# Binding the single-block split of a seven-product pair behind the split of the tile before it

## The chip, the cores and the metric

The kernel runs on one core of one Trainium2 chip. The metric is device time in microseconds (us) of one execution, given as the median of several executions. Of one execution there is also a profile, taken by the hardware profiler, from which all durations below come.

## The reference

One decoder layer in float32, on 272 tokens (16 meta tokens and 256 of the sequence) of width 2048. Two SwiGLU feed-forward blocks stand around a merge of a differential-attention mixer and a short convolution:

```
s = s + 0.5 * swiglu(rms_norm(s), ffn1)            # 2048 -> 2 x 5632 -> 2048
h = rms_norm(s);  q, k, v, b, c, u = split(h @ w_in)
gates = sigmoid(h @ w_gate)                        # 2048 -> 2 x 2048
merged = gates[0] * (y_att @ w_branch[0]) + gates[1] * (y_conv @ w_branch[1])
s = s + merged @ w_out
s = s + 0.5 * swiglu(rms_norm(s), ffn2)            # gate, up = split(h @ w_gu); (silu(gate) * up) @ w_down
return rms_norm(s)[16:]
```

The change touches how weights are prepared for `w_gate` and for ten of the eleven column groups of the second feed-forward's `w_gu`.

## The kernel before

**Precision by splitting.** TensorE multiplies in a reduced format (float32r). To keep float32 accuracy every operand is split into a high and a low part, and each product is made of three matmuls: high times high, low times high, high times low. For weights the split is done by `parts` (L384): ScalarE (ACT) casts the loaded weights to the high part `wh` (L392), and VectorE (DVE) subtracts to get the low part `wl` (L393). A "tile" below is one such split: 128 partitions by two blocks of 512 columns (a wide tile), or by one block of 512 (the single block).

**Direct and seven-product pairs.** `linear_mix` (L483) multiplies the activations, 256 tokens, by two column groups of 512. It goes through the 2048 rows of the weight in eight pairs of 128-row chunks. A direct pair (kind D) is eight products in two wide tiles, each with four products, so 12 matmuls for each tile. A seven-product pair (kind S) uses the Winograd form of Strassen's scheme: seven products on sums of blocks, in four tiles, in this order (L567 to L572):

- the single block, one product (3 matmuls),
- a wide tile of two loaded blocks, two products (6 matmuls),
- `t24`, two sums made on DVE by `sum24` (L538, L539), two products,
- `t13`, two sums, two products; in the second feed-forward they are made by an accumulating DMA on the GpSimd queue (`prefetch`, L543), in the gates by DVE (L531).

The kinds are `DDDSDSDS` for the gates (four passes of `linear_mix`) and `DDSDSSDS` for the second feed-forward (ten passes, column groups 1 to 10, taken in three groups of 3, 4 and 3 with the down projection behind each). That makes 12 and 40 single blocks, 52 in all.

**Buffers.** Loaded weights of a pair go into `st`, four buffers, by two DMAs on the SyncE (SP) queue (L526). The wide tiles' `wh` and `wl` rotate through three buffers each, so a wide cast can only start when TensorE has finished with the tile three places before. The single block has buffers of its own (tag `sc`, two buffers, one for `wh` and one for `wl`), so it doesn't wait for that rotation.

**What sets the order.** The program's text is not the order in which the engines run. A planner lays out each engine's queue from costs of its own: an instruction whose operands and buffers it takes to be ready goes ahead of earlier ones that still wait. On the chip each engine then runs its queue in that order. `tc.issue_after(ins)` binds: every instruction traced inside the block is put behind `ins` in the queue of `ins`'s engine. It was used here for `sum24` (L579), bound behind a given tile's subtraction. Matmuls are traced two wide tiles behind the splits (`step`, L246, AHEAD = 2).

At the end of a pass the eight PSUM results are combined on ACT and DVE (`done`, L588: L591 and L596 copy on ACT, L601 to L612 on DVE), and then SiLU and product (L622, L623). At the start of the next pass this work shares the two queues with the next pass's splits.

Of the kernel before, what the change touches and what calls it, by code (L numbers as in the profile page):

```python
# [9 lines left out]
F32 = mybir.dt.float32  # L10
# [41 lines left out]
def decoder_layer(ctx: ExitStack, tc: tile.TileContext, t, out):  # L52
    nc = tc.nc
# [46 lines left out]
    def load_gain(g0, src):  # L100
# [5 lines left out]
        out=vrows[G_CONV:G_SUB, :], in_=t["conv_w"][0].rearrange("k (c p) -> (k c) p", p=P)  # L106
# [3 lines left out]
    for i, n in enumerate(("lambda_q1", "lambda_k1", "lambda_q2", "lambda_k2")):  # L110
# [7 lines left out]
        out=mask[:, T - P :],  # L118
        in_=mask[:, T - P :],
# [126 lines left out]
    def step(use, ring=True):  # L246

        ahead.append((use, ring))
        while sum(r for _, r in ahead) > AHEAD:
            ahead.pop(0)[0]()  # L250
# [71 lines left out]
    def linear_tok(ops, chunks, k0, name, evict, side_at=(5, 9, 13), hold=0, after=None):  # L322
# [46 lines left out]
        for b, c in enumerate(chunks):  # L369
            if b % 2 == 0:  # L370
                st = wpool.tile([P, 2, 2, GW], F32, tag="st", bufs=ST_BUFS, name="st")
                r0 = (k0 + c) * P
                rows = [w[r0 : r0 + 2 * P, :].rearrange("(c p) f -> p c f", p=P) for w in (w0, w1)]
                if w1 is w0 and c1 == c0 + GW:
                    nc.sync.dma_start(out=st.rearrange("p c q f -> p c (q f)"), in_=rows[0][:, :, c0 : c0 + 2 * GW])
                else:
                    for q, cq in enumerate((c0, c1)):
                        nc.sync.dma_start(out=st[:, :, q, :], in_=rows[q][:, :, cq : cq + GW])
            wh, wl = parts(st[:, b % 2], held=b >= nk - hold)
            step(lambda b=b, wh=wh, wl=wl: use(b, wh, wl))  # L380

    split_last = [None]

    def parts(src, n=2, held=False):  # L384

        wh, wl = (
            tmp.tile([P, 1, GW], F32R, tag="sc", name=nm) if n == 1
            else (apool.tile([P, 2, GW], F32R, tag="act", name=nm) if held else wpool.tile([P, 2, GW], F32R, tag=nm, name=nm))
            for nm in ("wh", "wl")
        )  # L390
        wh, wl = wh[:, :n, :], wl[:, :n, :]
        nc.scalar.copy(out=wh, in_=src)  # L392
        split_last[0] = nc.vector.tensor_sub(wl, src, wh.bitcast(F32)).ins  # L393
        return wh, wl

    ng = F // GW
# [86 lines left out]
    def linear_mix(a, w, cols, name, done, fetch):  # L483
# [25 lines left out]
        def use(p, n, products):  # L509

            for k, left_op, wh, wl in products:
                product(k, left_op, wh, wl)
            if p == a.turn_at and later:
                later.pop(0)()
            if n == (1 if kinds[p] == "D" else 3):
                if p == 0:
                    flush()
                if side:
                    side.pop(0)()

        def load(p):

            st = wpool.tile([P, 2, 2, GW], F32, tag="st", bufs=ST_BUFS, name="st")
            rows = w[2 * p * P : (2 * p + 2) * P, :].rearrange("(c p) f -> p c f", p=P)
            for q in range(2):
                nc.sync.dma_start(out=st[:, :, q, :], in_=rows[:, :, cols[q] : cols[q] + GW])  # L526
            t13 = t24 = None
            if kinds[p] == "S":
                if not fetch:
                    t13 = wpool.tile([P, 2, GW], F32, tag="tt", bufs=2, name="t13")  # L530
                    nc.vector.tensor_add(t13, st[:, 0, :, :], st.rearrange("p c q f -> p q c f")[:, 1, :, :])  # L531
                t24 = wpool.tile([P, 2, GW], F32, tag="tt", bufs=2, name="t24")
            return st, t13, t24

        def sum24(k):
            st, t13, t24 = loaded[k]
            t13 = fetched.get(k, t13)
            nc.vector.tensor_add(t24[:, 0, :], t13[:, 0, :], st[:, 1, 1, :])  # L538
            nc.vector.tensor_add(t24[:, 1, :], t24[:, 0, :], st[:, 1, 0, :])  # L539
# [3 lines left out]
        def prefetch(p):  # L543
            t13 = fetched[p] = aux.tile([P, 2, GW], F32, tag="act", name="t13")
            rows = w[2 * p * P : (2 * p + 2) * P, :].rearrange("(c p) (q f) -> p c q f", p=P, q=2)
            fs = slice(cols[0], cols[0] + GW)
            nc.gpsimd.dma_start(out=t13, in_=rows[:, 0, :, fs])
            nc.gpsimd.dma_start(out=t13, in_=rows[:, :, 1, fs], accum_op=ALU.add)
# [3 lines left out]
        for p, kind in enumerate(kinds):  # L552
            if fetch:
                for k in range(0 if p == 0 else p + 4, min(p + 5, len(kinds))):
                    if kinds[k] == "S":
                        prefetch(k)
            st, t13, t24 = loaded[p]
            t13 = fetched.get(p, t13)
            (a11, a21), (a12, a22) = ([a.block(2 * p + c, i) for i in range(2)] for c in range(2))
            if kind == "D":  # L560
                tiles = [
                    (st[:, c], (("2", a1, 0), ("3", a1, 1), ("4", a2, 0), ("x", a2, 1)))
                    for c, (a1, a2) in enumerate(((a11, a21), (a12, a22)))
                ]
            else:
                s1, s2, s3, s4 = a.sums[p]
                tiles = [  # L567
                    (st[:, 1, 1:2, :], (("3", s4, 0),)),
                    (st[:, :, 0, :], (("1", a11, 0), ("2", a12, 1))),
                    (t24, (("6", s2, 0), ("4", a22, 1))),  # L570
                    (t13, (("5", s1, 0), ("7", s3, 1))),
                ]  # L572
            for n, (src, products) in enumerate(tiles):
                if n == 1 and p + far < len(kinds):
                    loaded[p + far] = load(p + far)
                wh, wl = parts(src, src.shape[1])
                if (p, n) in a.sums_at:

                    with tc.issue_after(split_last[0]):  # L579
                        sum24(a.sums_at[p, n])  # L580
                products = [(k, left_op, wh[:, j, :], wl[:, j, :]) for k, left_op, j in products]
                step(lambda p=p, n=n, products=products: use(p, n, products), src.shape[1] > 1)

    def mixed(a, w, cols, name, end, fetch=False):
# [3 lines left out]
        def done(k, ps):  # L588
# [21 lines left out]
            elif k == "7":  # L610
# [3 lines left out]
                pending.append(lambda: end(gt, up))  # L614

        linear_mix(a, w, cols, name, done, fetch)

    def gate_up_mix(a, w_gu, g, m, gi):
# [397 lines left out]
    for half in thirds:  # L1016
# [10 lines left out]
        if final:  # L1027
            for q in range(2):
                nc.gpsimd.dma_start(
                    out=gfin[q],  # L1030
                    in_=t["norm_final"][q * W2 : (q + 1) * W2].rearrange("(o d) -> o d", o=1).to_broadcast([P, W2]),
# [53 lines left out]
```

## Time and profile before

| quantity | value |
|---|---|
| time, median of 3 executions (range) | 2219.99 us (2218.17 to 2220.8) |
| time of the profiled execution | 2218.36 us |
| its span, first to last instruction | 2216.6 us (1.76 us lie around it) |
| mean granted TensorE clock | 0.996 |
| busy PE, DVE, ACT, POOL | 2183.6, 1469.3, 1058.2, 81.5 us |
| data moved | 443.91 MB, 200 GB/s on average |
| gates with their branch products | about 1122 to 1350 us of the span |
| ten passes of the second feed-forward, with the down projections | about 1500 to 2216 us |

How to read it: PE is TensorE's matmuls, PEld its weight loads. In a timeline row stand the start, the duration, the engine, the line, the operation, what is written and read, the shape, and in brackets how long the engine had been idle before it and what ended that. In a windows row stand a stretch, its length, the busy time and number of instructions of PE, PEld, DVE, ACT and POOL, then the granted TensorE clock, the mean busy share of the 16 DMA engines, and GB/s. A wait row names who waited for whom, us in total, how often, and the longest.

### The profile page before, as it was taken

The numbers are of one execution on the slowest core, as the hardware profiler recorded it, in microseconds if no ns is written. First come the engines' busy times: TensorE is split into PE (matmuls) and PEld (weight loads), VectorE is DVE, ScalarE is ACT, GpSimd is POOL, SyncE is SP. The second block draws the span as 40 slices with busy tenths as digits, with TensorE's granted clock in tenths as the row PEclk, the third lists the DMA queues.
The fourth block names the chain that finished last, engine by engine and source line by source line (L and its number), as shares of the span: only waits on it lengthen the run. The fifth ranks groups of instructions, "written<-read, shape, count | busy, mean of one in ns | idle before, by whom it ended". The sixth has DMA issues, their size and how long they took to land.

```text
span 2216.6 us, 33340 instructions
## 1 busy us (share of the span) xinstructions
PE 2183.6 (99%) x13504; PEld 1974.0 (89%) x13504; DVE 1469.3 (66%) x1919; ACT 1058.2 (48%) x1322; POOL 81.5 (4%) x97
## 2 busy tenths in 40 slices
PE   9999999999999999999999999999999999999998
PEld 8999999999999999898988888888778877887786
DVE  7555554455555565667897777679795678846885
ACT  6343343333433443444455555556563455534554
POOL 0000000000000000000000001000110011101100
PEclk9999999999999999999999999999999999999999
DMA  7455554555545555444555558556996699967973
GB/s 253 171 173 178 180 174 172 172 176 180 176 171 172 175 176 182 152 134 153 171 203 196 190 198 257 176 185 216 277 280 214 220 279 271 281 200 239 270 248 118
DMA packets 209034, 443.91 MB, mean 200 GB/s; under 512 B 9972, under 2 KB 10160, under 8 KB 208880
## 3 DMA queue, kind: packets, MB, share of 16 engines
q1 hardware_dynamic: 191232, 397.97, 52.4%
q0 software_dynamic: 17184, 43.16, 8.4%
q8 instruction: 105, 1.72, 0.3%
q10 hardware_dynamic: 464, 0.66, 0.1%
q14 instruction: 49, 0.40, 0.1%
HBM read 439.65 MB, written 2.10 MB: 199 GB/s over the span
## 4 chain that ended last, share of the span: by engine, by line
PE 92%; DMA 4%; DVE 2%; ACT 1%; issue 1%; SPq 0%; DVEq 0%; ACTq 0%
PE pg L505 4%; PE pu L297 4%; PE pd L297 4%; PE pd L295 4%; PE pu L295 4%; PE pu L296 4%; PE pd L296 4%; PE pg L504 4%; PE pg L503 4%; PE pg L297 4%; PE pg L295 4%; PE pg L296 4%; PE pd L337 4%; PE pd L335 4%; PE pd L336 4%; DMA st<-in_ffn_w_gu_dram 4%
## 5 line engine op out<-in xcount | busy, mean ns | idle before, releaser
L284 DVE TENSOR_TENSOR wl<-st,wh 128x1024 fp32r<-128x1024 f32 x392 | 478.9, 1224 | 453.3 <-ACT wh L283 452.8
L283 ACT CAST wh<-st 128x1024 fp32r<-128x1024 f32 x392 | 411.3, 1050 | 609.8 <-PE pd L296 146.9
L393 DVE TENSOR_TENSOR wl<-st,wh 128x1024 fp32r<-128x1024 f32 (+1 forms) x360 | 409.6, 1143 | 145.0 <-ACT wh L392 144.1
L392 ACT CAST wh<-st 128x1024 fp32r<-128x1024 f32 (+1 forms) x360 | 354.5, 991 | 300.1 <-PE pd L336 111.1
L295 PE MATMUL pg<-h,wh 128*128 128x272 f32 x704 | 203.0, 289 | 1.1 <-ACT wh L283 1.1
L295 PE MATMUL pu<-h,wh 128*128 128x272 f32 x704 | 203.2, 289 | 0.0
L297 PE MATMUL pu<-h,wl 128*128 128x272 f32 x704 | 203.1, 288 | 0.0
L297 PE MATMUL pd<-m,wl 128*128 128x272 f32 x704 | 203.0, 288 | 0.0
L295 PE MATMUL pd<-m,wh 128*128 128x272 f32 x704 | 203.0, 288 | 0.0
L296 PE MATMUL pd<-m,wh 128*128 128x272 f32 x704 | 202.5, 288 | 0.0
L296 PE MATMUL pu<-h,wh 128*128 128x272 f32 x704 | 202.4, 288 | 0.0
L296 PE MATMUL pg<-h,wh 128*128 128x272 f32 x704 | 201.8, 288 | 0.0
L297 PE MATMUL pg<-h,wl 128*128 128x272 f32 x704 | 200.5, 289 | 0.9 <-DVE wl L284 0.9
L393 DVE TENSOR_TENSOR wl<-t,wh 128x1024 fp32r<-128x1024 f32 x104 | 126.7, 1224 | 62.9 <-ACT wh L392 60.3
L392 ACT CAST wh<-t 128x1024 fp32r<-128x1024 f32 x104 | 108.6, 1051 | 122.9 <-PE pgx L504 76.2
L503 PE MATMUL pg<-wh,hn 128*128 128x512 f32 x360 | 143.3, 398 | 15.3 <-ACT wh L392 15.3
L505 PE MATMUL pg<-wl,hn 128*128 128x512 f32 x360 | 143.5, 399 | 4.4 <-DVE wl L393 4.4
L504 PE MATMUL pg<-wh,hn 128*128 128x512 f32 x360 | 142.3, 395 | 0.0
L335 PE MATMUL pd<-wh,m 128*128 128x512 f32 x352 | 137.6, 391 | 0.0
L337 PE MATMUL pd<-wl,m 128*128 128x512 f32 x352 | 137.1, 389 | 0.0
L336 PE MATMUL pd<-wh,m 128*128 128x512 f32 x352 | 137.0, 389 | 0.0
L295 PEld LDWEIGHTS pg<-h,wh 128*128 128x128 f32 x704 | 132.3, 188 | 1.8 <-ACT wh L283 1.8
(305 smaller groups left out, 4854.7 us busy)
## 6 DMA issues: line engine op xcount, KB each, us to landing
st<-in_ffn_w_gu_dram SPq DMA_DIRECT2D x184, 512.0 KB, 5.0
st<-in_ffn_w_down_dram SPq DMA_DIRECT2D x88, 1024.0 KB, 5.1
st<-in_ffn_w_gu_dram SPq DMA_DIRECT2D x84, 1024.0 KB, 4.9
st<-in_w_in_dram SPq DMA_DIRECT2D x48, 1024.0 KB, 5.1
t<-in_ffn_w_gu_dram POOLq DMA_DIRECT2D x80, 512.0 KB, 6.6
st<-in_w_gate_dram SPq DMA_DIRECT2D x64, 512.0 KB, 4.3
st<-in_w_branch_dram SPq DMA_DIRECT2D x32, 512.0 KB, 5.3
st<-in_w_out_dram SPq DMA_DIRECT2D x16, 1024.0 KB, 5.0
```

The source lines that it names most:

```text
L283: nc.scalar.copy(out=wh[:, :m, :], in_=sw)
L284: nc.vector.tensor_sub(wl[:, :m, :], sw, wh[:, :m, :].bitcast(F32))
L295: nc.tensor.matmul(a, wh[:, i, f], act.part(c, 0, t0, t1), start=first, stop=False)
L296: nc.tensor.matmul(a, wh[:, i, f], act.part(c, 1, t0, t1), start=False, stop=False)
L297: nc.tensor.matmul(a, wl[:, i, f], act.part(c, 0, t0, t1), start=False, stop=last)
L335: nc.tensor.matmul(ps, hi, wh[:, q, :], start=first, stop=False)
L337: nc.tensor.matmul(ps, hi, wl[:, q, :], start=False, stop=last)
L392: nc.scalar.copy(out=wh, in_=src)
L393: split_last[0] = nc.vector.tensor_sub(wl, src, wh.bitcast(F32)).ins
L503: nc.tensor.matmul(ps[k], hi, wh, start=first, stop=False)
L504: nc.tensor.matmul(ps[k], lo, wh, start=False, stop=False)
L505: nc.tensor.matmul(ps[k], hi, wl, start=False, stop=left[k] == 0)
```

## The change

`parts` keeps the last tile's two instructions (the cast on ACT and the subtraction on DVE) in `part_last`. When the tile is a single block (`n == 1`), its cast and its subtraction are traced with `issue_after` on both: the cast goes behind the preceding tile's cast on ACT, and the subtraction behind the preceding tile's subtraction on DVE. Nothing else is bound anew: `sum24` stays bound to the same subtraction under its new name. No instruction, buffer or transfer is added or taken away.

```
-    split_last = [None]
+    part_last = []
 
     def parts(src, n=2, held=False):
...
-        nc.scalar.copy(out=wh, in_=src)
-        split_last[0] = nc.vector.tensor_sub(wl, src, wh.bitcast(F32)).ins
+        with ExitStack() as order:
+            if n == 1 and part_last:
+
+                for ins in part_last:
+                    order.enter_context(tc.issue_after(ins))
+            part_last[:] = [nc.scalar.copy(out=wh, in_=src).ins]
+            part_last.append(nc.vector.tensor_sub(wl, src, wh.bitcast(F32)).ins)
         return wh, wl
...
-                    with tc.issue_after(split_last[0]):
+                    with tc.issue_after(part_last[1]):
                         sum24(a.sums_at[p, n])
```

## The prediction

> **What bounds the kernel now.** I read the page first: the span and the engines.
>
> ```profile
> span 2216.6 us, 33340 instructions
> PE 2183.6 (99%) x13504; PEld 1974.0 (89%) x13504; DVE 1469.3 (66%) x1919; ACT 1058.2 (48%) x1322; POOL 81.5 (4%) x97
> ```
>
> PE is the bound, and no work of PE's is removed. So the change can only be worth what PE loses now: idle time, and time at a lower clock. Next, therefore, the table of waits of PE, and of the stretch 1480 to 2100 for ACT:
>
> ```profile
> PE pg L503 <- ACT wh L392: 15.3, 7, 2.8
> PE pg L505 <- DVE wl L393: 4.4, 7, 0.7
> ...
> ACT wh L392 <- DMA st<-in_ffn_w_gu_dram: 27.7, 10, 4.1
> ```
>
> PE waits for weight splits seven times, 15.3 + 4.4 = 19.7 us. Both lines lie in `linear_mix`, and the splits are of `parts`. In the same stretch ACT waits for loads ten times. Whether the one makes the other is seen in the timelines of ACT and of PE around one such wait:
>
> ```profile
> 1820.33 1.05 ACT L392 CAST wh<-t 128x1024 fp32r<-128x1024 f32 x1 [1.71 <-PE pgx L504]
> 1823.05 1.05 ACT L392 CAST wh<-t 128x1024 fp32r<-128x1024 f32 x1 [1.67 <-PE pgx L504]
> 1824.00 0.58 ACT L591 COPY u2x<-pgx 128x512 f32<-128x512 f32 x1
> 1827.53 0.62 ACT L392 CAST wh<-st 128x512 fp32r<-128x512 f32 x1 [2.95 <-DMA st<-in_ffn_w_gu_dram]
> 1828.06 0.58 ACT L596 COPY cup<-pg 128x512 f32<-128x512 f32 x1
> 1828.53 2.94 ACT L392 CAST wh<-st 128x1024 fp32r<-128x1024 f32 x3
> 1833.40 1.06 ACT L392 CAST wh<-st 128x1024 fp32r<-128x1024 f32 x1 [1.93 <-PE pgx L504]
> ```
>
> ```profile
> 1824.64 0.39 PE L504 MATMUL pg<-wh,hn 128*128 128x512 f32 x1
> ...
> 1825.55 0.39 PE L505 MATMUL pg<-wl,sp 128*128 128x512 f32 x1
> ...
> 1827.36 0.39 PE L504 MATMUL pg<-wh,sp 128*128 128x512 f32 x1
> 1827.59 0.39 PE L505 MATMUL pg<-wl,sp 128*128 128x512 f32 x1
> 1829.63 0.50 PE L503 MATMUL pg<-wh,hn 128*128 128x512 f32 x1 [1.66 <-ACT wh L392]
> 1829.97 0.39 PE L504 MATMUL pg<-wh,hn 128*128 128x512 f32 x1
> 1830.20 0.40 PE L503 MATMUL pg<-wh,hn 128*128 128x512 f32 x1
> 1831.26 0.50 PE L505 MATMUL pg<-wl,hn 128*128 128x512 f32 x1 [0.67 <-DVE wl L393]
> 1831.59 0.40 PE L504 MATMUL pg<-wh,hn 128*128 128x512 f32 x1
> ```
>
> The 128x512 cast is a single block. It belongs to the third pair of the pass that starts here (the first S of `DDSDSSDS`), and it stands ahead of the four wide casts of the two direct pairs before it (the x3 row and the one at 1833.40). Its load landed only at 1827.5, so ACT stood for 2.95 us while the first direct tile, which PE needs first, was queued behind. That the three wide casts then run back to back, with no wait, shows that their data and buffers had been ready. So PE's wait is made by order alone.
>
> **What one such wait costs.** Matmuls follow each other every 0.23 us (1827.36 to 1827.59), though a row shows 0.39. From 1827.59 to 1829.63 are 2.04 us where 0.23 is due: 1.81 lost, against 1.66 shown as idle. The next interval, 0.34, loses 0.11; 1830.20 to 1831.26 loses 0.83, and the one after it (0.33) 0.10. That is 2.85 lost for 2.33 shown, 0.5 more. Over seven: 19.7 + 7 x 0.5 = 23.2 us.
>
> Then the clock. The windows view, asked for the 3.41 us shortly after four of the seven waits (first, last and sum of the four):
>
> ```profile
> 1565.89:1569.30 3.41, 3.41 (x10) 2.65 (x9) 3.41 (x5) 0.92 (x1) 0.43 (x1) 0.50 0.76 242
> ...
> 2098.37:2101.78 3.41, 3.04 (x7) 2.48 (x8) 3.41 (x6) 0.58 (x1) 0.00 (x0) 0.50 0.88 237
> sum 13.64, PE 12.33 PEld 9.28 DVE 13.64 ACT 3.57 POOL 0.43; mean PE 3.08 PEld 2.32 DVE 3.41 ACT 0.89 POOL 0.11
> ```
>
> ```profile
> 1566.44 0.63 PE L504 MATMUL pg<-wh,hn 128*128 128x512 f32 x1
> 1566.87 0.63 PE L505 MATMUL pg<-wl,hn 128*128 128x512 f32 x1
> ```
>
> The granted clock is 0.50 there, and matmuls come every 0.43 us instead of 0.23: 47% of PE's busy time is lost, 12.33 x 0.47 = 5.8 us. So the waits and their aftermath cost 23.2 + 5.8 = 29.0 us.
>
> The Trainium skill ("TensorE: Matmul & The Clock Gate", Why this matters for your kernels) sees a danger to the clock only in idle gaps of over about 3 us. By that rule gaps of 2.8 us and less would leave the clock alone, and the sum would be 23.2. The rows disagree, so the measurement decides; the 3.41 us itself is what the page gives as the length of the gate's window.
>
> **The change part by part.** *The bind on ACT.* At the seven places the single goes behind the fourth wide cast. The wide casts then start when their buffers come free. The rotation is three, so the first waits for the high part of the wide tile that PE leaves after 1824.64 (three tiles back), and starts at about 1824.9. With 1.05 it ends near 1826.0; PE needs it at 1827.59 + 0.23 = 1827.8. Its subtraction, next on DVE (1.22), would end by 1827.3 if DVE is free; PE wants it two matmuls later, at 1828.3. DVE is idle there:
>
> ```profile
> 1824.13 1.22 DVE L393 TENSOR_TENSOR wl<-t,wh 128x1024 fp32r<-128x1024 f32 x1 [1.49 <-ACT wh L392]
> 1828.18 0.69 DVE L393 TENSOR_TENSOR wl<-st,wh 128x512 fp32r<-128x512 f32 x1 [2.83 <-ACT wh L392]
> 1828.79 0.68 DVE L601 TENSOR_TENSOR cgate<-pg,cup 128x512 f32<-128x512 f32 x1
> 1829.39 0.68 DVE L603 TENSOR_TENSOR u2x<-pg,cup 128x512 f32<-128x512 f32 x1
> ```
>
> The copy L596, which now also stands behind the single, is free to go at about 1824.4, and L601 behind it. If L601 and L603 (0.60 each from start to start) both come ahead of the first subtraction, it ends at 1828.5, 0.2 late. So of each wait 0 to 0.2 us stays; I take the upper end, 7 x 0.2 = 1.4.
>
> *What is queued behind the single in its new place.* The other cast of the same pair, which needs the same load, and the two sums' casts. PE wants the single only after four direct tiles, 48 matmuls or 48 x 0.23 = 11.0 us into the pass. With 0.62 + 0.69 for its own split the load may land 9.7 us after the pass begins; it now lands 0.3 us before (1827.53 against 1827.8). So the same late load is covered.
>
> *The other singles.* Thirty in the second feed-forward follow a direct pair (three in each pass), and twelve in the gates; the ten that follow another S pair are kept in the order in which they are. Moving a single from ahead of a direct pair to behind it puts 0.53 us on ACT (1827.53 to 1828.06) and 0.61 on DVE (1828.18 to 1828.79) closer to the S pair's own three splits. On ACT it falls into the idle 1.71 ahead of 1820.33. On DVE:
>
> ```profile
> 1818.82 0.69 DVE L539 TENSOR_TENSOR t<-t,st 128x512 f32<-128x512 f32 x1
> 1819.42 1.22 DVE L393 TENSOR_TENSOR wl<-st,wh 128x1024 fp32r<-128x1024 f32 x1
> 1821.42 1.23 DVE L393 TENSOR_TENSOR wl<-t,wh 128x1024 fp32r<-128x1024 f32 x1 [0.78 <-ACT wh L392]
> ```
>
> ```profile
> 1139.64 1.23 DVE L393 TENSOR_TENSOR wl<-t,wh 128x1024 fp32r<-128x1024 f32 x1 [0.61 <-ACT wh L392]
> 1150.50 1.23 DVE L393 TENSOR_TENSOR wl<-t,wh 128x1024 fp32r<-128x1024 f32 x1 [1.20 <-ACT wh L392]
> ```
>
> The idle time ahead of `t24`'s subtraction (0.78 here, 0.61 and 1.20 in the gates) takes 0.61. If that cover were gone, PE still has a cushion: this subtraction ends at 1822.65, and PE uses it at 1825.55, 2.9 us later. Cost: nothing.
>
> *DMA.* No queue is passed by a transfer, but passes get shorter, so loads must come faster. The windows of two passes, and of a crowded stretch at a pass's end:
>
> ```profile
> 1783.80:1829.60 45.80, 43.75 (x188) 35.21 (x188) 37.94 (x44) 25.73 (x30) 7.46 (x8) 0.96 0.90 273
> 1829.60:1875.40 45.80, 42.35 (x188) 34.42 (x188) 37.97 (x44) 25.73 (x30) 7.43 (x8) 1.00 0.91 274
> 1771.00:1784.00 13.00, 10.72 (x48) 8.57 (x47) 7.29 (x9) 5.91 (x8) 3.42 (x4) 1.00 0.99 292
> ```
>
> A pass moves 274 x 45.80 = 12.5 MB. Without its loss (29.0 / 7 = 4.1) it takes 41.7 us, which asks for 301 GB/s, where 292 was moved at 0.99 busy. A shortfall of about 1 us a pass is possible; but at most four passes follow each other, and 9.7 us of slack were found above for the load that is late now. I count nothing, and keep the case as a rival.
>
> **Sum.** Against the profiled execution: 2218.36 - 29.0 + 1.4 = 2190.8 us (its span 2189.0 and the 1.76 around it). The profiled execution is 1.6 below the median, so the median becomes 2219.99 - 27.6 = 2192.4 us.
>
> **The rivals.** *DMA becomes the bound.* At 292 GB/s a pass takes 12.5 MB / 292 = 43.0 us: 2.8 saved instead of 4.1, 7 x 2.8 = 19.6, time 2200.4; with loads that crowd worse, half the gain, 2205. For it: 0.90 to 0.91 busy over whole passes. Against it: the slack, and that the DMA share has dips while loads wait for buffers, which earlier casts will release earlier. The Trainium skill ("DMA: Bandwidth & Descriptors", Specifications) gives a core about 358 GB/s from HBM, by which 12.5 MB would take 35 us and never bind; the 0.99 at 292 speaks against using that figure here, and the rival keeps its chance.
>
> *The time stays.* The first direct tile would start no earlier, because PSUM results of the old pass (L596, L601, L603, all late now too) hold what the new products need. Then the wait gets another name and the time is 2220. Against it: these three are late only because L596 stands behind the same single, as its start at the end of that cast shows.
>
> *Slower.* DVE gets the late engine in S pairs: if the single's 0.61 us isn't hidden, each of the 42 pairs behind a direct pair delays `t24` and makes PE wait 0.61, and with the extra 0.26 of a wait on `wl` (0.93 lost for 0.67 shown above) 0.87. That is 42 x 0.87 = 36.5 us, less the 29.0: 2227.5. It decides from the point where DVE's idle time ahead of `t24` is below 0.61 and PE's cushion of 2.9 is used up; at 0.61 to 1.20 the first is near in places, the second is not.
>
> **How the numbers follow.** Forecast 0.64; DMA as the bound 0.19; the time stays 0.08; slower 0.06; 0.03 for what I haven't thought of. Forecast and first rival hold 0.83. The low end is the full 29.0 with no remainder and 3 us for the median's own spread and the estimates: 2188. The high end is the first rival at its worse bound, 2205. A measurement of this kernel can tell about 0.2%, 4.4 us, from no change. Faster by more: the first two cases and half of the unknown, 0.84; within: 0.09; slower: 0.07.
>
> **What would show it.** In the changed kernel's profile: PE's waits for L392 and L393 nearly gone (under 3 us together); in ACT's timeline each single behind the wide casts; no half clock between 1480 and 2143; passes of 41.7 to 42 us instead of 45.8; ACT's waits for loads shorter than 27.7, since the single now asks later. If passes are near 43 us with PE waiting for splits that wait for loads, the first rival is right. If PE waits appear at `t24` or in the gates, the third is. A time of 2215 or more would say that the single's place was not the cause.

## The result, and the profile after

| | before | changed |
|---|---|---|
| median (range), 4 executions each | 2219.2 us (2218.17 to 2220.8) | 2194.07 us (2189.97 to 2195.52) |
| ratio, 95% interval | | 0.9883 (0.9866 to 0.9900) |
| span of the profiled execution | 2216.6 us | 2188.2 us |

The change saves 25.1 us in the medians (by the interval 22 to 30), and 28.4 us of span in the two profiled executions. 2192.4 had been forecast, 27.6 less than the 2219.99 of the three executions known then. Lines of the changed kernel stand five further down from `parts` on: the cast is L397, the subtraction L398, the matmuls L508 to L510, the end-of-pass work L596 to L628.

The page of the changed kernel, span and engines, and then the whole table of PE's waits:

```profile
span 2188.2 us, 33290 instructions
PE 2174.5 (99%) x13504; PEld 1971.0 (90%) x13504; DVE 1469.0 (67%) x1919; ACT 1057.1 (48%) x1322; POOL 81.6 (4%) x97
```

```profile
PE warm L75 <- POOL ident masks.py:199: 2.5, 1, 2.5
PE pg L295 <- ACT wh L283: 0.7, 2, 0.5
PE pg L510 <- DVE wl L398: 0.7, 2, 0.5
PE pg L297 <- DVE wl L284: 0.5, 2, 0.3
PE ssq_ps L211 <- DVE ssq L206: 0.2, 1, 0.2
```

DVE and ACT are as busy as before, to within 1.1 us, so no work went. The row in which PE waited 15.3 us for ACT's casts (L503, now L508) is gone, and the 4.4 us for subtractions is 0.7. ACT's wait for weight loads, 27.7 us before, no longer stands in its table at all. ACT's timeline at the start of the same pass, then PE's and DVE's:

```profile
1811.44 0.58 ACT L596 COPY u2x<-pgx 128x512 f32<-128x512 f32 x1
1812.05 0.59 ACT L601 COPY cup<-pg 128x512 f32<-128x512 f32 x1
1812.53 1.06 ACT L397 CAST wh<-st 128x1024 fp32r<-128x1024 f32 x1
1813.86 1.06 ACT L397 CAST wh<-st 128x1024 fp32r<-128x1024 f32 x1 [0.27 <-PE pg L509]
1815.22 1.06 ACT L397 CAST wh<-st 128x1024 fp32r<-128x1024 f32 x1 [0.30 <-PE pg L509]
1817.94 1.06 ACT L397 CAST wh<-st 128x1024 fp32r<-128x1024 f32 x1 [1.66 <-PE pgx L509]
1818.90 1.05 ACT L627 ACTIVATE cgate<-cgate 128x1024 f32<-128x1024 f32 x1
1819.86 0.60 ACT L397 CAST wh<-st 128x512 fp32r<-128x512 f32 x1
```

```profile
1815.02 0.39 PE L510 MATMUL pg<-wl,sp 128*128 128x512 f32 x1
1815.25 0.39 PE L508 MATMUL pg<-wh,hn 128*128 128x512 f32 x1
1815.48 0.39 PE L509 MATMUL pg<-wh,hn 128*128 128x512 f32 x1
1815.70 0.39 PE L510 MATMUL pg<-wl,hn 128*128 128x512 f32 x1
```

```profile
1812.80 0.69 DVE L606 TENSOR_TENSOR cgate<-pg,cup 128x512 f32<-128x512 f32 x1
1813.41 0.69 DVE L608 TENSOR_TENSOR u2x<-pg,cup 128x512 f32<-128x512 f32 x1
1814.02 1.22 DVE L398 TENSOR_TENSOR wl<-st,wh 128x1024 fp32r<-128x1024 f32 x1
```

The single (128x512) now stands behind four wide casts, and by then its load has landed: no bracket. The old pass's last matmul starts at 1815.02, the new pass's first at 1815.25; nothing is lost between passes. The first subtraction ends at 1815.24, 0.46 us before PE wants its result (1815.70). The windows of three passes, from pass start to pass start:

```profile
1773.40:1815.20 41.80, 41.80 (x189) 34.57 (x189) 38.00 (x45) 25.83 (x29) 7.89 (x10) 1.00 1.01 305
1815.20:1857.00 41.80, 41.80 (x189) 34.58 (x189) 38.09 (x45) 25.83 (x29) 6.28 (x7) 1.00 0.98 283
1857.00:1898.80 41.80, 41.28 (x186) 33.78 (x186) 36.90 (x44) 25.29 (x29) 7.46 (x8) 1.00 0.96 292
```

A pass takes 41.8 us in place of 45.8, the granted clock is 1.00, and the DMA share is 0.96 to 1.01. In the third PE misses 0.52 us. What is late there is new, as DVE's and PE's timelines show:

```profile
1877.81 0.69 DVE L543 TENSOR_TENSOR t<-t,st 128x512 f32<-128x512 f32 x1 [2.29 <-DMA t<-in_ffn_w_gu_dram]
```

```profile
1880.89 0.50 PE L510 MATMUL pg<-wl,hn 128*128 128x512 f32 x1 [0.52 <-DVE wl L398]
```

A sum of `sum24` waits on DVE for a prefetched block, and the subtractions queue behind it. The block is that of pair 5 (the pairs of a pass are counted 0 to 7, as in the code; `SUMS_FFN2` puts this sum behind the second tile of pair 3). DVE has four such waits in the ten passes here, three for pair 5 and one for pair 7, the last; in the profile of before it has none. The other wait of PE in the row for L398, under 0.2 us, stands behind the one for pair 7.

### The profile page after: what moved, and what is told of

The parts are those of the page before. It is cut to its first block, busy times and chain, and to the rows that moved or that the text cites. A ratio compares the mean times of both kernels' runs of the same rounds, so it can differ in the third digit from the quotient of the medians.

```text
span 2188.2 us, 33290 instructions
## 1 busy us (share of the span) xinstructions
PE 2174.5 (99%) x13504; PEld 1971.0 (90%) x13504; DVE 1469.0 (67%) x1919; ACT 1057.1 (48%) x1322; POOL 81.6 (4%) x97
## 4 chain that ended last, share of the span: by engine, by line
PE 97%; DVE 1%; DMA 1%; issue 1%; ACT 1%; SPq 0%; POOL 0%; DVEq 0%; POOLq 0%; ACTq 0%
PE pg L510 5%; PE pg L508 5%; PE pg L509 5%; PE pd L297 4%; PE pu L297 4%; PE pu L295 4%; PE pd L295 4%; PE pd L296 4%; PE pu L296 4%; PE pg L297 4%; PE pg L295 4%; PE pg L296 4%; PE pd L337 4%; PE pd L336 4%; PE pd L335 4%; PE o L293 3%
## 5 line engine op out<-in xcount | busy, mean ns | idle before, releaser
L398 DVE TENSOR_TENSOR wl<-st,wh 128x1024 fp32r<-128x1024 f32 (+1 forms) x360 | 409.3, 1144 | 137.0 <-ACT wh L397 136.2
L397 ACT CAST wh<-st 128x1024 fp32r<-128x1024 f32 (+1 forms) x360 | 349.9, 990 | 277.8 <-PE pd L336 116.6
L397 ACT CAST wh<-t 128x1024 fp32r<-128x1024 f32 x104 | 109.4, 1052 | 143.3 <-PE pgx L509 69.2
L398 DVE TENSOR_TENSOR wl<-t,wh 128x1024 fp32r<-128x1024 f32 x104 | 126.7, 1223 | 40.2 <-ACT wh L397 37.0
L510 PE MATMUL pg<-wl,hn 128*128 128x512 f32 x360 | 140.4, 390 | 0.7 <-DVE wl L398 0.7
L508 PE MATMUL pg<-wh,hn 128*128 128x512 f32 x360 | 140.5, 390 | 0.0
```

The costliest lines, as they stand in the source:

```text
L397: part_last[:] = [nc.scalar.copy(out=wh, in_=src).ins]
L398: part_last.append(nc.vector.tensor_sub(wl, src, wh.bitcast(F32)).ins)
L508: nc.tensor.matmul(ps[k], hi, wh, start=first, stop=False)
L510: nc.tensor.matmul(ps[k], hi, wl, start=False, stop=left[k] == 0)
```

## The experiments

Two theories stood at the start. The first: the gain comes from one place in ACT's queue, the cast of the first single of a pass, which waited there for a load. The rival: the order on DVE, or the many other bound singles, give part of it. A second question was open too: whether DMA, busy all the time, is the next bound. Some of the expectations take the late block to be the last pair's; in the profiles that of pair 5 is late more often. Each ratio is to runs of the kernel before on the same chip.

**The cast alone bound (e_act).** `for ins in part_last[:1]` in place of both.

> The changed kernel with the cast on ACT bound alone, and the subtraction on DVE left free. The planner lays out every queue just as in the changed kernel. Theory (the gain comes from the single's cast no longer standing ahead of the wide casts on ACT): same time as the changed kernel, 2190 to 2196 us, 0.988 of before, and PE's waits for splits under 3 us. It is also a second profile of the same order: if the first rival (DMA as the bound) has begun, some executions show a PE wait of 0.5 to 3 us in the fourth pass of the middle group, behind a DVE sum that waits for the prefetched block. Rival (both binds are needed): over 2200.

2192.44 us, ratio 0.9867 (0.9848 to 0.9886). The bind on DVE adds nothing: a subtraction waits for its cast in any case, and all queues come out alike. This is then a repetition of the changed kernel. In its profile PE waits 1.8 us for subtractions, three times, against 0.7 above.

**The subtraction alone bound (e_dve).** `for ins in part_last[1:]`.

> The subtraction on DVE bound alone, and the cast on ACT left free, so that the planner may put the cast ahead again. Theory: seven waits of PE for the wide casts, about 20 us shown and 25 to 29 lost, so 2215 to 2221 us. Rival (DVE's order is what matters, since DVE is the busier engine): the time of the changed kernel, 2190 to 2196.

2221.43 us, ratio 1.000 (0.9982 to 1.0018). DVE's queue is that of the changed kernel, and nothing is gained; six of the seven waits are back. PE's waits, and ACT at a pass's start:

```profile
PE pg L508 <- ACT wh L397: 12.5, 6, 2.7
PE pg L510 <- DVE wl L398: 4.7, 6, 0.8
```

```profile
1821.03 0.58 ACT L596 COPY u2x<-pgx 128x512 f32<-128x512 f32 x1
1824.75 0.62 ACT L397 CAST wh<-st 128x512 fp32r<-128x512 f32 x1 [3.14 <-DMA st<-in_ffn_w_gu_dram]
1825.28 0.58 ACT L601 COPY cup<-pg 128x512 f32<-128x512 f32 x1
1825.75 2.94 ACT L397 CAST wh<-st 128x1024 fp32r<-128x1024 f32 x3
```

The single is again ahead of the wide casts, and ACT stands for its load. With e_act this settles that ACT's order is what pays. PE's queue too came out a little different in the changed kernel: at each of the seven places two matmuls are swapped and a few transposes stand elsewhere. e_dve has the transposes' new place and gains nothing; the swap always came together with ACT's order and wasn't tried alone.

**Ten singles bound, and the other 42 (e_first, e_rest).** `parts` takes an argument, and binds only if it is true:

```
-                wh, wl = parts(src, src.shape[1])
+                wh, wl = parts(src, src.shape[1], bind=fetch and p == 2)        # e_first; e_rest: not (...)
```

> Only the first single block of each pass of the second feed-forward is bound (10 of 52), the one that stood ahead of four wide casts. Theory (only these cost time): the whole gain, 2190 to 2196 us, PE's waits for splits under 3 us. Rival (the other 42 places give or cost something): apart from the changed kernel by over 4 us either way.

> The other 42 single blocks are bound, and the first of each pass of the second feed-forward is free. Theory: nothing gained, 2215 to 2223 us, the seven waits of PE are back with 1.4 to 2.8 us each; after some of them, not after all, a spell of 3.41 us at half clock. Rival (the others give part of the gain): 2200 to 2212. Rival (the others cost): over 2225.

e_first: 2193.83 us, ratio 0.9877 (0.9853 to 0.9900), the whole gain as near as can be told. e_rest: 2218.34 us, ratio 0.9983 (0.9969 to 0.9998), a gain of at most 0.3%. So nearly all of the gain lies in the ten, and moving the other 42 costs nothing. Two things more are in these profiles. The profiled execution of e_first took 2199.67 us, longer than its other three (2191.13 to 2194.04); its DVE and PE show why:

```profile
2111.27 0.69 DVE L543 TENSOR_TENSOR t<-t,st 128x512 f32<-128x512 f32 x1 [5.38 <-DMA t<-in_ffn_w_gu_dram]
```

```profile
PE pg L510 <- DVE wl L398: 6.0, 5, 3.5
```

Here it is the block of pair 7 of the last pass, for which DVE stands 5.38 us. PE's waits, expected under 3 us, come to 6.0, and the clock is at 0.50 for 6.83 us from 2111.73 on. (e_first has the changed kernel's order on PE, but not on ACT and DVE.) And in e_rest two waits of PE of one length, and the 3.4 us behind each in the windows view, differ in the clock:

```profile
1782.40 0.51 PE L508 MATMUL pg<-wh,hn 128*128 128x512 f32 x1 [2.08 <-ACT wh L397]
...
1827.54 0.50 PE L508 MATMUL pg<-wh,hn 128*128 128x512 f32 x1 [2.06 <-ACT wh L397]
```

```profile
1784.50:1787.90 3.40, 3.40 (x17) 2.79 (x16) 3.40 (x6) 1.73 (x2) 0.80 (x1) 1.00 0.70 213
1829.90:1833.30 3.40, 3.40 (x9) 2.70 (x9) 3.40 (x5) 0.94 (x1) 1.17 (x1) 0.50 0.45 124
```

17 matmuls in the one, 9 in the other.

**Less to load (e_light, e_light_before).** The accumulating DMA of `prefetch` is cut short, in the changed kernel and in the kernel before. Both then leave out three quarters of the second summand:

```
-            nc.gpsimd.dma_start(out=t13, in_=rows[:, :, 1, fs], accum_op=ALU.add)
+            fq = slice(cols[0], cols[0] + P)
+            nc.gpsimd.dma_start(out=t13[:, :, :P], in_=rows[:, :, 1, fq], accum_op=ALU.add)
```

> The changed kernel with the prefetched sums cut short: the accumulating DMA adds only 128 of the 512 columns (so three quarters of each such sum lack their second block), which takes 4 x 0.39 = 1.6 MB out of the 12.5 MB of a pass. Theory (order was the whole cause, and what PE still loses comes from DMA at its limit): DVE no longer waits for prefetched blocks, PE's waits for splits under 0.5 us, 2187 to 2191 us. Rival (what is left comes from DVE's own crowd at the start of a pass): PE's waits stay, 2191 to 2195.

> The kernel before with the same sums cut short, the order free. Theory (the wait is order times lateness: the single stands ahead, and its load is late because 12.5 MB crowd a pass): the load lands 1 to 3 us earlier, the seven waits shrink to 0 to 1.5 us or go, 2190 to 2208 us. Rival (the single's place costs whatever the load does): still seven waits of 1.4 us and more, 2213 to 2222.

With the bind: 2189.45 us (2188.86 to 2191.54), ratio 0.9854 (0.9838 to 0.9869), and no wait of PE for `parts` left. With the order of before: 2200.53 us, ratio 0.9904 (0.9886 to 0.9921), between the two. PE's waits there:

```profile
PE pg L505 <- DVE wl L393: 4.6, 7, 0.7
PE pg L503 <- ACT wh L392: 2.8, 4, 1.0
```

Lighter loading took the casts' waits from 15.3 to 2.8 us, with the single still ahead. The seven short ones for subtractions (4.6) stayed. So the cost was order times lateness, and the lateness came from a crowd of loads. In the changed order DVE's waits for prefetched blocks are gone as well, with the three buffers of before.

**One load more (e_heavy).** The plain block of the first S pair is prefetched twice in each pass.

> The changed kernel with one load of 0.5 MB more in each of the ten passes: the plain block of the first seven-product pair is prefetched twice. Theory (DMA is at its limit in these passes): 13.0 MB at 306 GB/s is 42.5 us, 0.7 more than a pass takes, and the two loads follow each other on the queue, so sums wait for blocks and PE for splits: 2198 to 2220 us. Rival (the slack takes it): 2190 to 2197.

2191.88 us, ratio 0.9870 (0.9851 to 0.9888): no slower. Its windows of the first two of the three passes above:

```profile
1773.40:1815.20 41.80, 41.80 (x190) 34.58 (x189) 38.00 (x45) 25.83 (x30) 9.00 (x10) 1.00 1.04 318
1815.20:1857.00 41.80, 41.80 (x190) 34.58 (x189) 38.00 (x45) 25.84 (x30) 6.96 (x8) 1.00 1.01 308
```

318 GB/s, and PE without a gap in these passes. In all ten it has one wait for a split:

```profile
PE pg L510 <- DVE wl L398: 1.5, 1, 1.5
```

It stands behind a sum that waits 3.3 us for the block of pair 7 in the last pass. So bandwidth was not what is short at the rate of the changed kernel, and the expectation of 2198 and more was wrong. How much more would fit wasn't tried.

**One sum of each pass on DVE in place of DMA (e_mix).**

```
-                if not fetch:
+                if not fetch or p == 7:
...
-                    if kinds[k] == "S":
+                    if kinds[k] == "S" and k != 7:
```

> The changed kernel with the last pair's sum of each pass made on DVE (1.2 us each, ten times) in place of two DMAs, so 1.0 MB less a pass. Theory: no waits for prefetched blocks are left, and DVE has room for 1.2 us in 41.8: 2188 to 2192 us. Rival (DVE becomes the late engine in the last pair): PE waits for splits of the last pair, over 2196.

2198.4 us, ratio 0.9897 (0.9880 to 0.9913): slower than the changed kernel by the medians, though less is loaded. The ratios' intervals overlap; its five executions (2197.01 to 2202.48) lie above eleven of the twelve of the changed order, which ran on other chips. DVE's and PE's timelines:

```profile
1764.53 1.23 DVE L536 TENSOR_TENSOR t<-st 128x1024 f32<-128x1024 f32 x1 [4.80 <-DMA st<-in_ffn_w_gu_dram]
1765.67 1.22 DVE L398 TENSOR_TENSOR wl<-t,wh 128x1024 fp32r<-128x1024 f32 x1
```

```profile
1766.94 0.50 PE L510 MATMUL pg<-wl,sp 128*128 128x512 f32 x1 [3.72 <-DVE wl L398]
```

The new sum reads a fresh load, and the planner put it ahead of a subtraction that PE needed first. This is the fault of the kernel before once more, on another engine: DVE stands 4.80 us for the load and PE 3.72 behind it. The expectation had looked at DVE's room, not at its order.

**A fourth buffer for prefetched blocks (e_aux4, r_aux4, e_room), and the changed kernel again (r_after).** `N_AUX = 4`; the room comes from one buffer less for the norms' squares (e_aux4, r_aux4), or from moving the four lambda vectors into a buffer that is free at the start (e_room).

> The changed kernel with a fourth buffer for prefetched blocks (room made by one buffer less for the squares of the norms). Theory (the waits that are left come from the block of a pass's last pair, whose DMA must wait for a buffer): DVE's waits for prefetched blocks gone, 2188 to 2192 us, up to 4 us less than the changed kernel. Rival (DMA throughput is what is short): the waits only move, 2191 to 2196.

> The changed kernel once more, beside the next one on the same chip. Theory: 2190 to 2196 us; executions differ by a few us, since in some of them a sum on DVE waits longer for a prefetched block.

> The changed kernel with the fourth buffer for prefetched blocks once more, beside the changed kernel on the same chip. Theory: 1 to 3 us less than that, and executions closer together. Rival (no difference): within 1 us of it.

> The changed kernel with a fourth buffer for prefetched blocks, the room for it taken from a constant that is used only at the start, so that the planner's order on ACT, DVE, PE and SP stays that of the changed kernel. Theory (what PE still loses in the passes is the last pair's block, which waits for a buffer and not for DMA bandwidth): no wait of DVE's sums for prefetched blocks, no wait of PE for splits, 2188 to 2191 us, executions within 2 us of each other. Rival (bandwidth): the waits of DVE for prefetched blocks stay, 2190 to 2199.

e_aux4: 2191.3 us, ratio 0.9860 (0.9841 to 0.9878). Side by side, r_after took 2191.64 us (2190.41 to 2199.05) and r_aux4 2191.38 us (2190.91 to 2193.11): the medians are alike, the 1 to 3 us that were expected don't show, and only the one long execution is missing. e_room took 2189.26 us (2189.19 to 2191.48), ratio 0.9857 (0.9840 to 0.9873), with the changed kernel's order on ACT, DVE, PE and SP. DVE's waits in the passes, of r_after and then of e_room:

```profile
DVE wl L398 <- ACT wh L397: 125.0, 118, 1.8
DVE t L543 <- DMA t<-in_ffn_w_gu_dram: 7.9, 5, 2.5
DVE sT L1043 <- PE pd L337: 5.3, 4, 1.3
```

```profile
DVE wl L398 <- ACT wh L397: 128.4, 126, 1.5
DVE sT L1043 <- PE pd L337: 5.3, 4, 1.3
```

The wait for prefetched blocks is gone with a buffer alone, so these blocks were late because they had to start late. In the third pass shown above the accumulating transfer of pair 5 is issued 12.0 us after the pass's first matmul in the changed kernel, and 3.7 us after it in e_room. But e_light got there with three buffers: with less to move in the transfers ahead of it, the same transfer is issued after 3.5 us. Either a buffer or fewer bytes is enough; that it was the buffer alone isn't shown. e_room has the lowest median of the kernels here that compute the whole layer. Whether it beats the changed kernel stays open: the twelve executions of the changed order (its own four, e_act and r_after) lie between 2189.97 and 2199.05, and the intervals of the ratios overlap.

## Why the prediction was right

**The loss.** 15.3 + 4.4 us of idle time, the rest of each wait and the half clock were summed to 29.0. The span shrank by 28.4, and a pass takes 41.8 us where 41.7 was worked out. The clock term was real: no stretch at half clock is left in the passes of the changed kernel. It is the windows, 0.50 before and 1.00 after, that decide this. The Trainium skill ("TensorE: Matmul & The Clock Gate", Why this matters for your kernels) warns only of idle gaps over about 3 us. By that rule the clock term would be nothing, and the time, as an estimate, 2219.2 - 23.2 = 2196.0 us, above all four executions (2189.97 to 2195.52); the trace doesn't agree with it.

**What stays.** 0 to 0.2 us for each wait was allowed, at the first subtraction of a pass, with 1.4 in all. At that place nothing stayed: L606 and L608 both came ahead of the subtraction, as in the worse case, but earlier, since L601 no longer waited. (The worse case itself was 0.1 and not 0.2: 1826.0 + 1.22 is 1827.2, not 1827.3.) 0.7 us is shown as idle elsewhere, behind the late blocks of pairs 5 and 7. So that this term has about the right size is luck: its mechanism didn't occur, and another that the prediction put at nothing took its place. And that one varies: PE's waits for splits are 0.7, 1.8 and 0.6 us in the three profiles of the changed order (its own, e_act, r_after). The twelve executions of this order differ by up to 9 us; the long one, 2199.05, wasn't profiled. The long one that was, of e_first, had waited for the block of pair 7.

**The other singles** cost nothing, as forecast (e_rest, if anything a gain of up to 0.3%).

**DMA.** As a rival it was priced at 43.0 us a pass, from 292 GB/s at 0.99 busy. That price was wrong: 318 GB/s at 1.04 fits into 41.8 us. A busy share near 1 in a crowded stretch was read as a ceiling, and it isn't one. Nothing was counted for DMA because of 9.7 us of slack, but that slack was worked out for the single's load alone. What did appear is the lateness of the prefetched blocks, which a fourth buffer (e_room) or lighter transfers (e_light) take away.

**Time stays, and slower.** The PSUM results were late only through the single, as argued; DVE's crowd in the S pairs reached PE only where a sum had waited for a prefetched block.

**Median against profile.** The profiled execution of the changed kernel was the fastest of its four, so the median's gain, 25.1, is less than the span's, 28.4. Both lie in the ratio's interval.

## What to carry to other kernels

An instruction with buffers of its own is free to run early, so a planner will put it early; on a queue that runs in order that is a risk whenever it waits for a load, because all that is queued behind it then waits for the same load. Look for an engine's wait for a DMA, see what stands behind it in its queue and which engine needs that first, and bind the early one behind it. The same fault came back on DVE in e_mix when a new reader of a fresh load was added, so look again after each change.

## What the hardware showed that was not expected

- Whether a wait of PE is followed by 3.41 us at half clock is not settled by its length: in e_rest 2.06 us was and 2.08 us was not. Over the profiles of before, e_dve and e_rest 10 of 20 waits were (4 of 7, 3 of 6, 3 of 7), with 2.8 us as the longest idle time. In e_light_before two short ones were enough (1.01 and 0.67 us; from 1866.40 on the clock is 0.50):

```profile
1864.05 0.50 PE L503 MATMUL pg<-wh,hn 128*128 128x512 f32 x1 [1.01 <-ACT wh L392]
1865.67 0.50 PE L505 MATMUL pg<-wl,hn 128*128 128x512 f32 x1 [0.67 <-DVE wl L393]
1866.53 0.63 PE L503 MATMUL pg<-wh,hn 128*128 128x512 f32 x1
```

- What does sort them is the idle time within one stretch of a fixed grid. The four half-clock stretches of before begin at 1565.89, 1784.35, 1876.51 and 2098.37, which is 64, 27 and 65 times 3.413 us apart, and the steps in the other profiles are whole multiples too. Laid on that grid from 1480 to 2150 us, in before, e_act, e_dve, e_rest, e_light_before, e_first, e_heavy and e_mix, every stretch at full clock with more than 2.0 us of PE idle (8 of 8) was followed by half clock, none with less than 1.6 was, and between 1.68 and 1.92 it was 6 of 10. So short waits close together add up, and the same wait costs more or less by where it falls. What decides in the range between is open.
- The busy share of the DMA engines reads 1.01 at 305 GB/s and 1.04 at 318, so a share near 1 is no sign that the limit of the rate is reached, and dividing the rate by it gives no limit.
